# The first load of a streaming cosine-similarity kernel, split into four strided transfers

## Chip, core, metric

One core of one Trainium2 chip. The metric is the device time of one launch in microseconds; the median over runs is given.

## What is computed

For 8192 rows of 8192 float32 values in x and y, the cosine of each pair of rows:

```python
x_norm = np.linalg.norm(x, axis=1, keepdims=True)
y_norm = np.linalg.norm(y, axis=1, keepdims=True)
return np.sum(x * y, axis=1) / (x_norm.squeeze() * y_norm.squeeze() + 1e-8)
```

Each element is used once or twice and never again: 537 MB have to be read, and nothing can be reused.

## The kernel before

The core streams x and y through three buffers of 128 partitions x 64 KB ("slots"). A group is 256 rows, 2 rows per partition, so that each partition receives one unbroken run of 65,536 bytes. ScalarE squares and sums, VectorE multiplies and sums x*y, TensorE only relays semaphores in the loop. The first load is moved by a hook into the program's opening block, ahead of the opening barrier, so that the stream begins as early as it can. The parts that matter (cuts marked):

```python
def first_load_and_last_wait(nc):
    ...
    load = next(i for i in body.instructions if i.opcode == "DMACopy")
    assert not load.sync_info.on_wait
    ...
    body.instructions = [i for i in body.instructions if i.name != load.name]
    opening.instructions = head[:at] + [load] + head[at:]
...
def load(src, m):
    return nc.sync.dma_start(out=slots[m % SLOTS], in_=src).then_inc(landed[m % SLOTS], 16)
...
load(xg[0, 0], 0)          # 128 partitions x 64 KB: moved ahead of the opening barrier
load(yg[0, 0], 1)
load(xg[0, 1], 2)
...
with nc.tensor.Fori(0, R):
    for m in range(2 * SLOTS):
        take(nc.tensor, landed[m % SLOTS], 16)
        nc.tensor.sem_inc(for_act, 1)
        nc.tensor.sem_inc(for_dve, 1)
```

Of the kernel before, what the change touches and what calls it, by code (L numbers as in the profile page):

```python
# [15 lines left out]
def first_load_and_last_wait(nc):  # L16


    blocks = nc.m.functions[0].blocks
    body = next(b for b in blocks if any(i.opcode == "DMACopy" for i in b.instructions))  # L20
    load = next(i for i in body.instructions if i.opcode == "DMACopy")
    assert not load.sync_info.on_wait
    opening = blocks[0]
    head = list(opening.instructions)
    at = 1 + next(n for n, i in enumerate(head)
                  if i.opcode == "ISA" and i.engine == load.engine)
    body.instructions = [i for i in body.instructions if i.name != load.name]
    opening.instructions = head[:at] + [load] + head[at:]



    closing = blocks[-1]
    for b in blocks:
        waits = [i for i in b.instructions
                 if i.sync_info and any(
                     "stored" in (w.ant_name or "") for w in i.sync_info.on_wait)]
        if waits:
            b.instructions = [i for i in b.instructions if i.name not in {w.name for w in waits}]
            closing.instructions = waits + list(closing.instructions)
# [25 lines left out]
def kernel(  # L65
# [5 lines left out]
):  # L71
    nc = tc.nc
    nc.at_finalize(first_load_and_last_wait)
    P = nc.NUM_PARTITIONS
    n_rows, K = x.shape
# [13 lines left out]
    xg = x[0:G * 2 * P, :].rearrange("(r a p j) k -> r a p (j k)", a=SLOTS, p=P, j=2)  # L89
# [17 lines left out]
    slots = [sb.tile([P, 2 * K], FP32, name=f"slot{s}") for s in range(SLOTS)]  # L107
# [18 lines left out]
    def sem(name):  # L126
        return tc.alloc_semaphore(name)

    landed = [sem(f"landed{s}") for s in range(SLOTS)]
    for_act, for_dve = sem("for_act"), sem("for_dve")  # L130
    squared, x_squared, y_squared, partial, used = (
# [6 lines left out]
    def take(engine, s, n=1):  # L138
        engine.wait_ge(s, n).then_inc(s, -n)  # L139
# [9 lines left out]
    def load(src, m):  # L149
        return nc.sync.dma_start(out=slots[m % SLOTS], in_=src).then_inc(landed[m % SLOTS], 16)  # L150
# [16 lines left out]

    with tc.tile_critical():  # L168

        load(xg[0, 0], 0)  # L170
        load(yg[0, 0], 1)
        load(xg[0, 1], 2)

# [8 lines left out]
            load(src[g // SLOTS, g % SLOTS], m)  # L182


        with nc.tensor.Fori(0, R):
            for m in range(2 * SLOTS):
                take(nc.tensor, landed[m % SLOTS], 16)
                nc.tensor.sem_inc(for_act, 1)
                nc.tensor.sem_inc(for_dve, 1)
# [18 lines left out]
        with nc.vector.Fori(0, R) as r:  # L208
# [20 lines left out]
            out=ident, in_=ident, compare_op=ALU.not_equal, fill=1.0, base=0,  # L229
# [42 lines left out]
        def flat(t):  # L272
            return t.rearrange("p q r c -> p q (r c)")
# [10 lines left out]
        for b in range(NB):  # L284
# [8 lines left out]
            for n, p in enumerate(pieces[b]):  # L293
# [4 lines left out]
                else:  # L298
                    dve.wait(*marks)
                    m_base = dve.done(nc.vector.tensor_reduce(  # L300
                        out=base, in_=parts, axis=AX.X, op=ALU.add))
# [24 lines left out]
                if b == last and n == 4:  # L326
# [3 lines left out]
                        out=bnorm[:, :, 0:last], in_=bsum[:, 0:2, 0:last], func=ACTF.Sqrt))  # L330
                    m_den = reciprocal(bnorm[:, :, 0:last], bden[:, 0:last], m_norm, m_sum)
            if b in manys and b != last:
                dve.wait(*marks)
                m_sum = dve.done(nc.vector.tensor_reduce(
                    out=bsum[:, :, b:b + 1], in_=parts, axis=AX.X, op=ALU.add))
            freed[b] = marks
            if b == 0:
# [3 lines left out]
                    out=gnorm, in_=flat(gsum)[:, 0:2], func=ACTF.Sqrt))  # L341
# [3 lines left out]
                    out=gden, in0=flat(gsum)[:, XY], in1=gden))  # L345
                rows = []
                for j in range(2):
# [3 lines left out]
                        out=t, in_=gden[:, j:2 * G:2], identity=ident))  # L351
# [3 lines left out]
            if b == 2:  # L355
                act.wait(*rows)
                nc.scalar.dma_start(
                    out=out[0:G * 2 * P].rearrange("(g q) -> g q", q=2 * P),
                    in_=orow.rearrange("g p j -> g (p j)")).then_inc(stored[0], 16)
# [4 lines left out]
            out=bnorm[:, 0, last:], in_=base[:, XX:XX + 1], func=ACTF.Sqrt))  # L364
        act.wait(m_fin)
        m_yn = act.done(nc.scalar.activation(
            out=bnorm[:, 1, last:], in_=fin, func=ACTF.Sqrt, bias=base[:, YY:YY + 1]))
# [6 lines left out]
            out=bden[:, last:], in0=bnorm[:, 1, last:], scalar1=bnorm[:, 0, last:],  # L374
# [10 lines left out]
            out=out.rearrange("(t p) -> t p", p=P)[nt - NB:, :], in_=orl).then_inc(  # L385
# [33 lines left out]
```

## Time and profile before

| | before |
|---|---|
| time, median of 6 runs | 1249.34 us (1249.20 to 1249.48) |
| span of the profiled run | 1247.6 us |
| share of the span that the load queue keeps 16 DMA engines busy | 99.6% |
| ACT, DVE busy | 73%, 56% |
| one run of 64 KB on one DMA engine (median of 7,680 records) | 2.420 us |

Two things to know for reading what follows. A DMA engine's record is one run of 64 KB (7,680 records of 65,536 bytes; the last blocks are cut smaller, and a semaphore write has a record of its own, 4 bytes and 8 to 14 ns in the kernel before), and in the windows view a record counts, with its whole length and all its bytes, in the window in which it starts. So in a window that contains the starts of just 16 runs, one per engine, the mean length of a run is the DMA share times the width of the window, and the number of runs is GB/s times the width divided by 65.5 KB. And a share above 1.00 in a narrow window is therefore no error. Lengths of single runs, where the text names them, are from the same transfer records of the trace.

### The profile page before, as it was taken

Reading aid. Unit: us, or ns where it says so; the run is one execution under the profiler, and the core shown is the slowest. Engines: PE = TensorE matmul, PEld = TensorE weight load, DVE = VectorE, ACT = ScalarE, POOL = GpSimd, SP = SyncE. Lnnn points to the kernel's source line nnn. Section 1 sums busy time; section 2 is a strip of 40 time slices with the busy share of each in tenths; the row PEclk is TensorE's granted clock in tenths of the full one; section 3 lists DMA queues with packets and bytes.
Section 4 is the critical chain, followed back from the end, with each engine's and each line's share of the span. In section 5 each row is a group of like instructions: output and inputs, shape, how many; then the busy total and the mean of one; then the engine's idle time right before and its main releaser. Section 6 shows DMA issues by size and latency. Waiting matters only on the chain. (4 is left out here: it accounts for less than half of the span.)

```text
span 1247.6 us, 1785 instructions
## 1 busy us (share of the span) xinstructions
PE 1.3 (0%) x4; PEld 0.3 (0%) x4; DVE 698.2 (56%) x252; ACT 916.9 (73%) x285; POOL 0.8 (0%) x8
## 2 busy tenths in 40 slices
PE   0000000000000000000000000000000000000000
PEld 0000000000000000000000000000000000000000
DVE  1654576545765447654467544675446755457566
ACT  3686776867768668677686776867868668677888
POOL 0000000000000000000000000000000000000000
DMA  9999999999999999999999999999999999999998
GB/s 435 431 414 435 437 437 437 437 435 435 433 412 437 437 437 437 437 437 435 435 424 420 437 437 437 437 437 437 433 433 412 437 437 437 437 437 437 418 425 335
DMA packets 11575, 536.93 MB, mean 430 GB/s; under 512 B 1299, under 2 KB 1845, under 8 KB 2613
## 3 DMA queue, kind: packets, MB, share of 16 engines
q1 hardware_dynamic: 11528, 536.88, 99.6%
q10 hardware_dynamic: 45, 0.03, 0.0%
q14 instruction: 2, 0.02, 0.0%
HBM read 536.87 MB, written 0.03 MB: 430 GB/s over the span
## 5 line engine op out<-in xcount | busy, mean ns | idle before, releaser
L142 ACT ACTIVATE junk<-slot 128x8192 uint8<-128x8192 f32 (+4 forms) x138 | 900.8, 6528 | 326.2 <-ACTq L139 320.5
L145 DVE CUSTOM_DVE_ANT_0 slot<-slot,slot 128x4096 f32<-128x4096 f32 (+1 forms) x60 | 391.1, 6556 | 452.4 <-DVEq L139 452.4
L212 DVE COPY side<-slot 128x4096 f32<-128x4096 f32 x30 | 132.8, 4428 | 71.7 <-DVEq L139 71.7
L145 DVE CUSTOM_DVE_ANT_0 side<-side,slot,part 128x4096 f32<-128x4096 f32 x30 | 134.6, 4488 | 0.0
L145 DVE CUSTOM_DVE_ANT_0 slot<-slot 128x8192 f32<-128x8192 f32 (+3 forms) x5 | 29.6, 5944 | 20.4 <-ACT junk L142 12.7
L142 ACT ACTIVATION_READ_ACCUMULATOR junk<-slot (+1 forms) x138 | 25.7, 186 | 0.0
L145 DVE CUSTOM_DVE_ANT_0 vjunk<-slot 128x384 uint8<-128x384 f32 (+4 forms) x8 | 6.8, 886 | 1.0 <-DMA slot<-in_y_dram 1.0
L145 DVE DVE_READ_ACCUMULATOR2_ANT gsum<- x60 | 6.7, 112 | 0.0
L145 DVE DVE_READ_ACCUMULATOR2_ANT part<- 128x1 f32 x30 | 2.5, 83 | 0.0
L192 ACT ACT_TABLE_LOAD x1 | 1.3, 1283 | 1.0 <-SPq L168 1.0
L350 PE MATMUL side<-ident,gden 128*30 128x128 f32 x2 | 0.6, 395 | 1196.9 <-DVE gden L344 1196.9
L194 ACT ACT_TABLE_LOAD x1 | 1.3, 1283 | 0.1
L145 DVE DVE_READ_ACCUMULATOR2_ANT parts<- 128x1 f32 x11 | 0.9, 82 | 0.0
L353 DVE COPY orow<-side 30x128 f32<-30x128 f32 x2 | 0.5, 279 | 0.6 <-PE side L350 0.6
L371 ACT COPY dots<-side 4x128 f32<-4x128 f32 x1 | 0.3, 254 | 0.7 <-PE side L369 0.7
L145 DVE CUSTOM_DVE_ANT_0 vjunk<-slot,base 128x384 uint8<-128x384 f32 x1 | 0.6, 619 | 0.1
L381 DVE TENSOR_TENSOR orl<-side,dots 4x128 f32<-4x128 f32 x1 | 0.3, 279 | 0.5 <-PE side L379 0.5
L270 DVE RECIPROCAL gden<-gden 128x60 f32<-128x60 f32 x1 | 0.5, 529 | 0.0
L350 PEld LDWEIGHTS side<-ident,gden 128*30 128x30 f32 x2 | 0.1, 107 | 1196.8 <-issue 1196.8
L369 PE MATMUL side<-ident,bsum 128*4 128x128 f32 x1 | 0.4, 373 | 46.9 <-DVE bsum L145 46.9
L379 PE MATMUL side<-ident,bden 128*4 128x128 f32 x1 | 0.4, 374 | 0.0
L340 ACT ACTIVATE gnorm<-gsum 128x120 f32<-128x120 f32 x1 | 0.3, 302 | 0.0
(25 smaller groups left out, 4.4 us busy)
## 6 DMA issues: line engine op xcount, KB each, us to landing
slot<-in_x_dram SPq DMA_DIRECT2D x3, 4096.0 KB, 29.9
slot<-in_y_dram SPq DMA_DIRECT2D x2, 4096.0 KB, 32.2
slot<-in_y_dram SPq DMA_DIRECT2D x1, 2368.0 KB, 35.8
slot<-in_x_dram SPq DMA_DIRECT2D x1, 1984.0 KB, 32.3
slot<-in_y_dram SPq DMA_DIRECT2D x1, 1728.0 KB, 39.4
slot<-in_y_dram SPq DMA_DIRECT2D x1, 1600.0 KB, 35.7
slot<-in_x_dram SPq DMA_DIRECT2D x1, 1088.0 KB, 37.9
slot<-in_y_dram SPq DMA_DIRECT2D x1, 640.0 KB, 40.2
```

Of the source, the lines that this page charges most:

```text
L142: return nc.scalar.activation(out=into, in_=src, func=ACTF.Square, accum_out=acc)
L145: return nc.vector.tensor_tensor_reduce(out=into, in0=a, in1=b, scale=1.0, scalar=init, op0=ALU.mult, op1=ALU.add, accum_out=acc)
L192: nc.scalar.memzero(dummy).then_inc(squared, 1)
L194: nc.scalar.sqrt(out=dummy, in_=dummy).then_inc(squared, 1)
L212: nc.vector.tensor_copy(out=side, in_=xt[:, CUT:])
L270: return dve.done(nc.vector.reciprocal(out=den, in_=den))
L340: m_norm = act.done(nc.scalar.activation(out=gnorm, in_=flat(gsum)[:, 0:2], func=ACTF.Sqrt))
L350: mk = pe.done(nc.tensor.transpose(out=t, in_=gden[:, j:2 * G:2], identity=ident))
L353: rows.append(dve.done(nc.vector.tensor_copy(out=orow[:, :, j], in_=t)))
L369: m_xy = pe.done(nc.tensor.transpose(out=psl[0], in_=bsum[:, XY, :], identity=ident))
L371: m_dots = act.done(nc.scalar.copy(out=dots, in_=psl[0]))
L379: mk = pe.done(nc.tensor.transpose(out=psl[1], in_=bden, identity=ident))
```

## The change

A load of 128 partitions is 128 runs, 8 for each of the 16 DMA engines: the 16 semaphore writes of the first load come at 20.97 to 21.57 us, at the end of the eighth generation of 16 runs, and ACT's first square follows at 22.36. The change wants the engines to start sooner by giving each only one run in the first transfer, then one, two and four more. The transfers are strided; each engine is meant to stay within a set of 8 partitions of its own by that. They are partitions 0, 8, .. 120; then 4, 12, .. 124; then 2, 6, .. 126; then 1, 3, .. 127. Three of them count on a semaphore of their own, for which TensorE waits once.

```diff
-    load = next(i for i in body.instructions if i.opcode == "DMACopy")
+    loads = [i for i in body.instructions if i.opcode == "DMACopy"][:4]
...
-    opening.instructions = head[:at] + [load] + head[at:]
+    opening.instructions = head[:at] + loads + head[at:]
...
+    first = sem("first")
...
-        load(xg[0, 0], 0)
+        for start, step in ((0, 8), (4, 8), (2, 4), (1, 2)):
+            nc.sync.dma_start(
+                out=slots[0][start::step], in_=xg[0, 0, start::step]).then_inc(
+                    landed[0] if step == 2 else first, 16)
...
+        nc.tensor.wait_ge(first, 48)
         with nc.tensor.Fori(0, R):
```

More of the change, by code (lines that the diff above doesn't have):

```diff
@@ L20, in first_load_and_last_wait @@
     body = next(b for b in blocks if any(i.opcode == "DMACopy" for i in b.instructions))
-    load = next(i for i in body.instructions if i.opcode == "DMACopy")
-    assert not load.sync_info.on_wait
+    loads = [i for i in body.instructions if i.opcode == "DMACopy"][:4]
+    assert not any(i.sync_info.on_wait for i in loads)
     opening = blocks[0]
@@ L25, in first_load_and_last_wait @@
     at = 1 + next(n for n, i in enumerate(head)
-                  if i.opcode == "ISA" and i.engine == load.engine)
-    body.instructions = [i for i in body.instructions if i.name != load.name]
-    opening.instructions = head[:at] + [load] + head[at:]
+                  if i.opcode == "ISA" and i.engine == loads[0].engine)
+    body.instructions = [i for i in body.instructions if i.name not in {k.name for k in loads}]
+    opening.instructions = head[:at] + loads + head[at:]
     closing = blocks[-1]
```

## The prediction

Passages that no trace or run of this case bears out are cut from the text, and the cuts are marked. Two of its numbers stand as estimates alone: that a first transfer with an eighth of the runs would win half of the measured loss of 0.87 us and a little more, 0.5 us; and that the runs of rival 2, the "conflict" of its last paragraphs, would take twice the measured 2.42 us, 4.84 us. That a faster stream isn't to be had was not shown either; the prediction counts on none.

> **What bounds the kernel now.** I read the page first. Every one of the 40 slices of the span has the DMA engines at 90% or more except the last, while DVE is busy 56% and ACT 73%; the queue of the loads holds 99.6% of the time of 16 engines:
>
> ```profile
> span 1247.6 us, 1785 instructions
> DMA  9999999999999999999999999999999999999998
> q1 hardware_dynamic: 11528, 536.88, 99.6%
> HBM read 536.87 MB, written 0.03 MB: 430 GB/s over the span
> ```
>
> Next, the table of windows over the loop (columns that matter here: the stretch in us, and at the end of the line the DMA share and GB/s; a transfer record counts in the window in which it starts). Share 1.00 in all: no engine waits for a free buffer anywhere in the loop. So time can be won only before the stream of loads runs, by a faster stream, or after it.
>
> ```profile
> 25.00:325.00 300.00, 0.00 (x0) 0.00 (x0) 167.17 (x53) 222.84 (x63) 0.00 (x0) 1.00 1.00 433
> 325.00:625.00 300.00, 0.00 (x0) 0.00 (x0) 165.87 (x55) 218.48 (x63) 0.00 (x0) 1.00 1.00 433
> ```
>
> The DMA records of the trace give the unit: a run of one partition (2 rows of x, 65,536 bytes) is one record, 7,680 of them, median 2.420 us, which is 27.1 GB/s for one of 16 engines. All of x and y is 536.87 MB / 65,536 / 16 = 512 such runs per engine, 512 x 2.420 = 1239.0 us. Of the span of 1247.6 us only about 8.6 us is anything else.
>
> The change touches the head. The timeline and the fine windows of it:
>
> ```profile
> 0.00 0.41 SPq L150 DMA_DIRECT2D slot<-in_x_dram  x1
> 1.07 0.33 SPq L150 DMA_DIRECT2D slot<-in_y_dram  x1
> 22.36 7.03 ACT L142 ACTIVATE junk<-slot 128x8192 uint8<-128x8192 f32 x1 [18.25 <-ACTq L139]
> ```
>
> ```profile
> 1.00:1.25 0.25, 0.00 (x0) 0.00 (x0) 0.00 (x0) 0.23 (x1) 0.20 (x1) 1.00 8.78 2884
> 1.25:1.50 0.25, 0.00 (x0) 0.00 (x0) 0.00 (x0) 0.25 (x1) 0.02 (x2) 1.00 3.04 1049
> 1.75:2.00 0.25, 0.00 (x0) 0.00 (x0) 0.00 (x0) 0.25 (x1) 0.13 (x3) 1.00 0.62 262
> 4.00:4.50 0.50, 0.00 (x0) 0.00 (x0) 0.00 (x0) 0.11 (x1) 0.00 (x0) 1.00 4.54 1966
> 4.50:5.00 0.50, 0.00 (x0) 0.00 (x0) 0.00 (x0) 0.00 (x0) 0.00 (x0) 1.00 0.30 131
> ```
>
> Read the first line so: 2884 GB/s x 0.25 us = 0.72 MB = 11 runs begin there; their time is 8.78 x 0.25 x 16 = 35.1 us, 3.19 us each. Four more begin by 1.50 (3.04 us each), and the sixteenth engine begins only at 1.98 and needs 2.48. From the second run on (15 begin before 4.50: 4.54 x 0.5 x 16 / 15 = 2.42 us) everything runs at 2.42. So the first runs take up to 1.0 us more than any later ones. By the records the engines begin their second runs between 4.06 and 4.66 us, mean 4.33. Had all begun at 1.04 and taken 2.42, it would be 3.46: the head loses **0.87 us in the mean and 1.20 on the last engine**, and the last one matters, since a load has landed only when all 16 have.
>
> Last, the end, where the chain of waits and the timeline of ACT show that a shift of the stream is a shift of the end: the last blocks wait for DMA, and then compute runs on without a gap.
>
> ```profile
> 1222.16 19.49 DMA slot<-in_y_dram
> 1241.65 0.02 issue
> 1241.67 0.54 DVE vjunk L145
> ```
> ```profile
> 1237.89 1.27 ACT L142 ACTIVATE junk<-slot 128x1280 uint8<-128x1280 f32 x1 [0.26 <-DMA slot<-in_y_dram]
> ```
>
> [...] The trace of before has no addresses. What it does show is that engines phase-locked within 0.6 us all run at 27.1 GB/s[...].
>
> **The change part by part.**
> - Three more issues at the start. An issue of 128 runs took 0.33 to 0.52 us of SP; four take about 1.5 us instead of 0.41, so the opening barrier falls some 1.1 us later, and so do the ACT table loads (from 1.02) and the issues of y and the second x (from 1.07). Needed: y's descriptors at about 21 us, ACT at 22.36. Slack 19 us: **0**. A queued run lasts 2.42 us, far longer than the 0.4 us to the next issue, so no engine runs dry between the four: **0**.
> - Semaphore writes: one per engine and transfer, records of 9 ns. Three more: **+0.03 us**.
> - TensorE waits once for 48 before its loop. The fourth transfer is queued last on every engine and so ends last; the wait is long over or ends with it: under 0.1 us, and that on a consumer, not on the stream: **0**.
> - The gain. Fifteen engines start at 1.04 to 1.44 and yet end their first run 0.5 to 1.0 us late, the sixteenth starts 0.9 us late and is not slowed. [...] Possible is at most the 0.87 mean, 1.20 last. [...] I take half of the mean and a little more for the last engine: **-0.5 us**.
> Sum: 1249.4 - 0.5 + 0.03 = **1248.9 us**.
>
> **The rivals.**
> 1. *The slowness of the first runs is a cold start[...].* Against it: the engine that started last took 2.48. For it: that one started when the others were already warm. Then the gain is 0 to 0.2: 1249.2 to 1249.4.
> 2. [...] the first two transfers, and in step the third and fourth too, run [...] 4.84 instead of 2.42 us a run. All 8 runs: +19.4 us, **1268**; only the first two: +4.8 us, **1254**. Nothing later can win this back, since the stream has no slack. [...] Against it: the change is made so that each engine keeps its 8 partitions, which somebody seems to have had reason for[...]. I give this 4 in 10.
> 3. *The load is hidden anyway*, as ACT waits for it only at 22.36: rejected, because it's the stream, not that wait, that sets the end.
>
> **Range and chances.** Without a conflict 1248.2 (all of 1.2 us) to 1249.5; with one 1254 to 1269. The point is where the more likely branch lies, 1248.9; a range for 8 in 10 has to hold the other branch as well, 1248.2 to 1268.5. 2% faster would be 1224.4, under the 1239.0 of the runs alone: 0.01. 2% slower is 1274.4, beyond even the full conflict: 0.03. Within 2%: 0.96.
>
> **What would show it.** Right: in the fine windows all first runs begin by about 1.5 us and last nearer 2.4 than 3.2; the second runs begin at 3.6 to 4.2; ACT's first square begins at about 21.8 instead of 22.36; the final DVE pieces are 0.5 us earlier. Cold start: first runs still about 3.1 us. Conflict: runs of about 4.8 us and half of 437 GB/s up to 10 us or to 40 us, ACT's first square near 27 to 41, and the whole timeline late by the same. What would make the prediction wrong otherwise: issues of strided transfers that cost much more than 0.5 us on SP, so that engines run dry between them, or runs cut into smaller pieces by the stride.

## The result, and the profile after

| | before | after |
|---|---|---|
| time, median of 6 runs each | 1249.34 us | 1254.67 us (1254.42 to 1254.92) |
| span of the profiled run | 1247.6 us | 1252.5 us |
| load queue, share of 16 engines | 99.6% | 99.6% |

The ratio is 1.0043, 95% interval 1.0030 to 1.0056. It is the mean time of one kernel's runs over that of the other's of the same rounds, so not quite the ratio of the medians. The change costs 5.3 us: within 2%, outside the noise, and in the direction that was not the point of the prediction.

The page's busy row does not show where. The DMA engines are "90% or more" in 39 of 40 slices in both kernels. The row below it does. This is its GB/s row for the kernel before (its DMA row is in the prediction), then both rows for the kernel after (slices of about 31 us):

```profile
GB/s 435 431 414 435 437 437 437 437 435 435 433 412 437 437 437 437 437 437 435 435 424 420 437 437 437 437 437 437 433 433 412 437 437 437 437 437 437 418 425 335
```
```profile
DMA  9999999999999999999999999999999999999998
GB/s 362 427 429 427 433 433 435 435 435 435 435 435 435 435 435 435 433 433 435 425 429 427 435 431 435 435 435 435 435 435 435 435 435 435 435 433 433 413 429 335
```

The first slice moved 362 GB/s instead of 435, by engines that the page has at 90% or more all the time: (435 - 362) x 31.3 us = 2.3 MB less, and 2.3 MB at 435 GB/s is 5.3 us. The fine windows of the kernel after, one for each generation of 16 runs:

```profile
1.40:1.90 0.50, 0.00 (x0) 0.00 (x0) 0.00 (x0) 0.00 (x0) 0.00 (x0) 1.00 9.61 2097
5.60:6.90 1.30, 0.00 (x0) 0.00 (x0) 0.00 (x0) 0.85 (x2) 0.00 (x0) 1.00 3.79 807
10.50:11.80 1.30, 0.00 (x0) 0.00 (x0) 0.00 (x0) 0.00 (x0) 0.00 (x0) 1.00 2.29 807
13.80:14.70 0.90, 0.00 (x0) 0.00 (x0) 0.00 (x0) 0.00 (x0) 0.00 (x0) 1.00 2.69 1165
```

Each line has 16 runs (2097 x 0.50 / 65.5 = 16, and so on). The runs of the first transfer take 9.61 x 0.50 = 4.80 us, those of the second 4.91 (the window gives 3.79 x 1.30 = 4.93 and includes the short semaphore writes), the first ones of the third transfer 2.96 (2.98 by the window, again with semaphore writes), and from then on 2.42 as before (2.69 x 0.90 = 2.42). So two transfers, the two of 16 partitions, ran at half rate (4.80 and 4.91 us a run beside 2.42). By the records the account is complete: mean start of the first runs 1.54 us instead of 1.23 (+0.31), first run 4.80 instead of 3.11 (+1.69), second 4.91 instead of 2.42 (+2.49), third 2.96 instead of 2.42 (+0.54), sum 5.03 us. The rest of the kernel is the old one, later. Here are the issues and ACT's first square, and the end of the chain, of the kernel after:

```profile
0.00 2.53 SPq L173 DMA_DIRECT2D slot<-in_x_dram  x4
3.42 0.39 SPq L151 DMA_DIRECT2D slot<-in_y_dram  x1
27.61 7.03 ACT L143 ACTIVATE junk<-slot 128x8192 uint8<-128x8192 f32 x1 [21.14 <-ACTq L140]
```
```profile
1225.38 21.24 DMA slot<-in_y_dram
1246.62 0.02 issue
1246.64 0.54 DVE vjunk L146
```

ACT starts 27.61 - 22.36 = 5.25 us later, the final DVE pieces 1246.64 - 1241.67 = 4.97 us later. Of the profiled pair's difference in time (1254.58 - 1249.41 = 5.17 us) and of the medians' 5.33, the 4.97 us leave some 0.2 to 0.4 us that are not placed by the trace.

### The profile page after: what moved, and what is told of

Its sections match the earlier page's. It is cut to its first block, busy times and chain, and to the rows that moved or that the text cites. A ratio compares the mean times of both kernels' runs of the same rounds, so it can differ in the third digit from the quotient of the medians.

```text
span 1252.5 us, 1788 instructions
## 1 busy us (share of the span) xinstructions
PE 1.3 (0%) x4; PEld 0.3 (0%) x4; DVE 698.2 (56%) x252; ACT 916.9 (73%) x285; POOL 0.8 (0%) x8
## 3 DMA queue, kind: packets, MB, share of 16 engines
q1 hardware_dynamic: 11576, 536.88, 99.6%
```

## The experiments

Theory: how long a run takes depends on which partitions the transfer writes, and two sets of 16 partitions 8 apart (0, 8, .. 120 and 4, 12, .. 124) are slow ones. Rivals: small transfers are slow as such; rows that are read 512 KB apart are slow to read.

The expectations named theories of why a set of partitions is slow, and from them said which runs would be slow. No trace of this case shows the mechanisms, so they are cut, with the cuts marked. What is left of an expectation are the lengths and times that it said, estimates in multiples of the measured 2.42 us; where two or three alternatives follow each other, each belonged to a theory of its own.

### Three transfers, of 32, 32 and 64 partitions

```diff
-        for start, step in ((0, 8), (4, 8), (2, 4), (1, 2)):
+        for start, step in ((0, 4), (2, 4), (1, 2)):      # and 3 hoisted loads, wait for 32
```

> First load in three strided transfers, partitions 0,4,..,124 then 2,6,..,126 then 1,3,..,127 (32, 32, 64)[...]. [...] no run of about 4.9 us is left, the first runs take about 3 us and all later ones 2.42; time 1248.8 to 1250, that is 4.7 to 5.9 us under the changed kernel. Rival, small transfers as such are slow (their set-up or their completion): the two first transfers still cost about 2 us per run, some 1252 to 1255. Rival, rows read from DRAM at a pitch of 512 KB collide: the pitch is now 256 KB, which that theory leaves open; no clear expectation.

Measured: 1250.11 us (5 runs, 1249.78 to 1250.26) beside 1249.32 for the kernel before, ratio 1.0006 with an interval of 0.9992 to 1.0019. Correct. The windows of its first two generations:

```profile
1.30:2.30 1.00, 0.00 (x0) 0.00 (x0) 0.00 (x0) 0.00 (x0) 0.00 (x0) 1.00 3.09 1049
4.40:5.00 0.60, 0.00 (x0) 0.00 (x0) 0.00 (x0) 0.60 (x1) 0.00 (x0) 1.00 4.05 1748
```

First runs 3.09 us, second 2.43: the half-rate runs are gone with the transfers of 16 partitions 8 apart, and about 4.6 us with them. Of the 0.8 us that are left over the kernel before, the trace places 0.34: the mean start of the second runs is 4.67 us instead of 4.33, and as the first runs are no longer than before, it is the stream that starts later. This already says that the gain hoped for does not exist either: with 2 runs per engine in the first transfer instead of 8, the first run takes as long as ever (3.09, before 3.11).

### The same sizes, adjacent partitions

```diff
-        for start, step in ((0, 8), (4, 8), (2, 4), (1, 2)):
-            ... out=slots[0][start::step], in_=xg[0, 0, start::step] ...
+        for lo, hi in ((0, 16), (16, 32), (32, 64), (64, 128)):
+            ... out=slots[0][lo:hi], in_=xg[0, 0, lo:hi] ...
```

> First load in the same four sizes (16, 16, 32, 64) but of adjacent partitions: 0 to 15, 16 to 31, 32 to 63, 64 to 127. [...] a run takes about 4 x 2.42 = 9.7 us in the first two transfers; the third and fourth [...] 4.84 us a run. Sum 9.7 + 9.7 + 9.7 + 19.4 = 48.5 us instead of 19.4 for the load: about 1278, at least 1265[...]. Rival, small transfers as such are slow: the same as the changed kernel, 1254 to 1255, runs of 4.9 us. Rival, DRAM pitch of 512 KB: rows now lie 64 KB apart, so 1249 to 1250.

Measured: 1278.99 us (4 runs), ratio 1.0238, interval 1.0222 to 1.0254. The windows, one for each of the first four generations:

```profile
1.00:1.80 0.80, 0.00 (x0) 0.00 (x0) 0.00 (x0) 0.00 (x0) 0.00 (x0) 1.00 10.57 1311
8.60:10.30 1.70, 0.00 (x0) 0.00 (x0) 0.00 (x0) 0.00 (x0) 0.00 (x0) 1.00 5.48 617
17.90:19.60 1.70, 0.00 (x0) 0.00 (x0) 0.00 (x0) 0.00 (x0) 0.00 (x0) 1.00 3.34 617
24.00:25.00 1.00, 0.00 (x0) 0.00 (x0) 0.00 (x0) 0.00 (x0) 0.00 (x0) 1.00 5.12 1049
```

10.57 x 0.80 = 8.46 us for the first run, 9.29 by the records for the second, 5.6 and 5.1 after that, in the transfer of 32 adjacent partitions. Expected were 9.7, 9.7, then 4.84. A run of 16 adjacent partitions takes 3.8 times 2.42 us in the second transfer, one of 32 adjacent partitions 2.1 to 2.3 times. The whole is 29.7 us slower; the expectation had said about 29. Sizes and count of the transfers are those of the changed kernel. But two things differ from it, the partitions and the rows of DRAM that are read; the next run has the rows of this one with the partitions of the changed kernel, and the comparison of the two is the strongest single result.

### The same partitions, adjacent rows of DRAM

```diff
+        for start, step, lo, hi in ((0, 8, 0, 16), (4, 8, 16, 32), (2, 4, 32, 64), (1, 2, 64, 128)):
+            ... out=slots[0][start::step], in_=xg[0, 0, lo:hi] ...
```

> The changed kernel's partitions of SBUF (0,8,.. then 4,12,.. then 2,6,.. then 1,3,..), but each transfer reads adjacent rows of DRAM[...]. The rows of the first group are then wrong on purpose (256 of 8192 results). [...] nothing changes, runs of 4.9 us in the first two transfers, time 1254 to 1255.5. Rival, DRAM pitch: runs of 2.4 to 3.1 us, time 1249 to 1250.[...]

Measured: 1254.57 us (4 runs), the same as the changed kernel. Its output is wrong, which doesn't matter for the time. The windows of its first two generations:

```profile
1.40:2.20 0.80, 0.00 (x0) 0.00 (x0) 0.00 (x0) 0.00 (x0) 0.00 (x0) 1.00 5.91 1311
5.70:6.70 1.00, 0.00 (x0) 0.00 (x0) 0.00 (x0) 0.77 (x2) 0.00 (x0) 1.00 5.01 1049
```

First runs 5.91 x 0.80 = 4.73 us, second 4.99 by the records. Where the rows are read from makes no difference to the time (1254.57 and 1254.67 us): the DRAM rival is out. The rival of small transfers as such allows this time, but for the run of adjacent partitions, of the same sizes, it had said 1254 to 1255 us. And beside the run of adjacent partitions, which reads the same rows with transfers of the same sizes, only the partitions written differ: 1278.99 us there, 1254.57 here. What it is about the partitions that costs the time, these runs don't show.

### Probes

The other nine runs are the kernel before with one extra transfer into the third buffer, whose own load then waits for it. For example:

```diff
         load(xg[0, 0], 0)
+        nc.sync.dma_start(out=slots[2][0:106:7], in_=xg[0, 1, 0:106:7]).then_inc(probed, 16)
         load(yg[0, 0], 1)
+        nc.sync.wait_ge(probed, 16)
         load(xg[0, 1], 2)
```

The extra runs stand in the records right behind the first load, at 21 us, when all engines run in step at 2.42 us. All probes give right results. Their times, 1252 to 1258 us, include the extra bytes and the wait and say little; one look each, so their state is unknown, but the verdict is in lengths of single runs, which are steady at 2.42 us elsewhere in the same trace.

**16 partitions 7 apart from 0**:

> The kernel before, with one extra transfer of 16 partitions 7 apart (0, 7, .., 105) into the third buffer right behind the first load, when the engines already run in step; the third buffer's own load waits for it. [...] of the 16 extra runs exactly 4 take clearly more than 2.42 us (up to 4.9), 12 take 2.42. Rival, small transfers as such: all 16 equally slow. Rival, DRAM pitch (448 KB here): none slow, or all. The time itself says little: the extra 1 MB and the wait cost at least 2.4 us.

A miss:

```profile
20.80:21.60 0.80, 0.00 (x0) 0.00 (x0) 0.00 (x0) 0.00 (x0) 0.00 (x0) 1.00 5.30 1311
```

All 16 runs took 3.8 to 4.6 us, mean 4.23 by the records, where 4 slow and 12 fast ones had been expected. I formed two other theories, and the next probes were to tell them apart; their mechanisms stayed without evidence.

**8 partitions, 4 apart from 0**, the control:

> The probe of 16 partitions 7 apart slowed all 16 runs (3.8 to 4.6 us)[...]. This probe is the control: an extra transfer of 8 partitions 4 apart (0, 4, .., 28)[...]. [...] the 8 extra runs take 2.42 us and nothing is slow. If they are slow all the same, then a transfer of few partitions is slow as such.

All 8 extra runs, and the other engines' runs beside them, took 2.42 us:

```profile
21.00:21.70 0.70, 0.00 (x0) 0.00 (x0) 0.00 (x0) 0.00 (x0) 0.00 (x0) 1.00 3.47 1498
```

3.47 x 0.70 = 2.43 us with the semaphore writes. Few partitions alone do no harm.

**8 partitions, 4 apart from 4**:

> As the control, with partitions 4, 8, .., 32[...]. [...] the 8 extra runs take clearly more than 2.42 us, 3.5 to 4.9. [...] 2.42 us, apart from up to 0.7 us at the start[...].

The runs at that moment took 2.44 to 2.57 us, the next 2.57 to 2.77. Nothing near 3.5: of the 1.1 us and more that the first alternative added to 2.42, some 0.2 are to be seen (0.35 in the slowest run).

**8 partitions, 5 apart from 0**:

> As the control, with partitions 0, 5, .., 35[...]. [...] all 8 extra runs take 3.8 to 4.9 us, and perhaps the other 8 engines' first runs of y too. [...] 4 runs of 2.42 us and 4 slow ones. [...] 2 slow runs, 6 of 2.42.

Exactly two runs were slow, 4.14 and 4.22 us; six took 2.42, and so did the other eight engines. The windows show it by the starts of the next runs:

```profile
21.00:21.50 0.50, 0.00 (x0) 0.00 (x0) 0.00 (x0) 0.00 (x0) 0.00 (x0) 1.00 5.29 2097
23.50:23.90 0.40, 0.00 (x0) 0.00 (x0) 0.40 (x1) 0.40 (x1) 0.00 (x0) 1.00 5.33 2294
25.20:25.50 0.30, 0.00 (x0) 0.00 (x0) 0.30 (x1) 0.30 (x1) 0.00 (x0) 1.00 1.22 437
```

Sixteen begin by 21.5; fourteen (2294 x 0.40 / 65.5) go on before 23.9 and two (437 x 0.30 / 65.5) after 25.2. That is the third alternative, which neither of my two new theories had expected.

**16 partitions, 3 apart from 0**:

> 16 partitions 3 apart (0, 3, .., 45)[...]. [...] all 16 runs take [...] about 6.5 to 7.3 us. [...] as in the probe 7 apart, so about 4.2 us as there. [...] 3 runs near 2.4, 4 near 4.8, 9 near 7.3.

All 16 were slow:

```profile
21.00:21.50 0.50, 0.00 (x0) 0.00 (x0) 0.00 (x0) 0.00 (x0) 0.00 (x0) 1.00 14.50 2097
```

They took 6.7 to 7.8 us, mean 14.50 x 0.50 = 7.25, three times 2.42 (7.26). Here the first alternative was right, all of them slow, though it was not with 8 partitions.

**16 partitions, 4 apart from 28**:

> The extra transfer behind the first load again, 16 partitions 28, 32, .., 88[...]. [...] all 16 runs take 3.8 to 4.9 us[...]. [...] as with 8 partitions: 2 slow runs, 14 of 2.4 to 2.7.

Two slow runs, 5.0 and 5.5 us, and fourteen of 2.7 to 2.9. That is nearest to the second alternative, but the rest lost too, and more in their next runs: 13 of the 14 that followed took 3.1 to 3.3 us and one 5.08.

**16 partitions, 7 apart from 11** (spacing of the first probe):

> As before, 16 partitions 7 apart from 11 on (11, 18, .., 116): the same spacing as the probe in which all runs were slow[...]. [...] 2.4 to 2.7 us, no run over 3. [...] all about 4.2 us, as in the probe 7 apart from 0.

No slow run at all:

```profile
21.00:21.60 0.60, 0.00 (x0) 0.00 (x0) 0.00 (x0) 0.00 (x0) 0.00 (x0) 1.00 4.05 1748
```

4.05 x 0.60 = 2.43 us in the mean, with the spacing and the number of partitions of the probe that took 4.23. The second alternative is refuted, and so is "16 partitions are slow as such". What separates the two probes is the start, and with it the partitions that are written (the rows that are read made no difference above), and nothing else that I varied.

**16 partitions, 4 apart from 24**:

> Open since the other probes: [...] slows two runs of 16, [...] (7 apart from 0) and [...] (3 apart) slowed all 16. [...] with the spacing of the one that behaved: 24, 28, .., 84[...]. [...] 4 slow runs of 4 to 5.5 us, 12 of 2.4 to 2.8. [...] all 16 take 3.8 to 5 us. Which it is, no theory of mine says beforehand.

All 16 slow, 4.1 to 4.8 us:

```profile
20.90:21.50 0.60, 0.00 (x0) 0.00 (x0) 0.00 (x0) 0.00 (x0) 0.00 (x0) 1.00 7.51 1748
```

7.51 x 0.60 = 4.51 us. Beside the probe from 28 only one partition of the sixteen is another, 24 for 88 (the others have moved up a place in the transfer), and there two runs were clearly slow and here all sixteen. Each was seen in one transfer only. Why, I can't say; no run here tells it, and it stays open. The changed kernel doesn't depend on it: its own two sets were measured, 4.80 and 4.91 us.

**16 partitions, 4 apart from 32, ahead of everything**: 32, 36, .. 92, issued before the first load.

> What the change meant to do[...]: an extra transfer of 16 partitions, 32, 36, .., 92[...], into the third buffer, ahead of everything. Theory COLD START: the first run on every engine is slow[...] however little is queued behind it; the 16 runs take 2.9 to 3.4 us (2.4 for an engine that begins late), as the first runs of the kernel before. Theory of the prediction[...]: they take about 2.4 us[...]. Both: none takes 4.2 to 5.4 us as the first runs of the changed kernel did, though this too is a transfer of 16 partitions.

```profile
1.40:2.20 0.80, 0.00 (x0) 0.00 (x0) 0.00 (x0) 0.74 (x1) 0.47 (x3) 1.00 3.73 1311
```

3.73 x 0.80 = 2.98 us in the mean, with most of the early starters between 2.9 and 3.4. COLD START had the lengths right: one run per engine does not start up quicker than eight (2.98 and 3.11 us). The prediction's estimate, that with fewer runs in the first transfer the first one gets shorter, had not. The run is what the change wanted to do, done without runs of 4.2 us and more (all next runs begin by 5.1 us), and it wins nothing; it also begins at 1.41 us instead of 1.04.

One rival is not met by this run alone. The hook moves only the extra transfer, so the full loads are issued right behind it (SP is busy with them from 1.51 to 2.37 us), and it could be that work that slows the first runs. The records speak against it: the four engines that began at 1.98 us or later, beside the second of these issues, took 2.49 to 2.76 us, and in the kernel before, where full loads are issued at 55.31 and 59.99 us into the running stream, the runs of that moment take 2.42 to 2.43. What it is that is cold in the first microseconds, no run tells.

No version came out that beats the kernel before. The best split, 32, 32 and 64, is 0.8 us behind in the medians; by the interval that is within noise, though all five of its runs lie above all nine of the kernel before. A split needs a gain from the first run, and there is none.

## Why the prediction was right or wrong

The measured 1254.67 us lies in the range; the point, 1248.9, is 5.8 us off, on the wrong side of the kernel before. By its own steps:

- **The bound**: right. The loop of the kernel after has a share of 1.00 and 433 GB/s as before, and what the head lost, nothing won back. (The full slices of the page before run from 412 to 437 GB/s; the 300 us windows, 433, are the better figure.)
- **Three more issues, cost 0**: half right. They cost more than the 1.5 us estimated, 2.53 us on SP for the four (0.57 to 0.64 each by the records, before 0.41), and the ACT table loads moved from 1.02 to 3.37 us. That was hidden, as said. What was not hidden is that the first data came later, mean start 1.54 us instead of 1.23: +0.31 us, a term missing from the sum. It goes with the length of the first issue: 0.64 us here and the first data at 1.42; 0.42 us and 1.03 with adjacent partitions.
- **Semaphore writes, TensorE's wait**: right, nothing to see (records of 8 to 20 ns). The semaphore writes of the four transfers come at 5.65 to 6.86, 10.56 to 11.78, 16.27 to 17.04 and 25.94 to 26.71 us: the fourth does end last, and what TensorE waits for is there 9.7 us before the load's end.
- **The gain of 0.5 us**: this step failed. It was the estimate that fewer runs in the first transfer would make the first run shorter: the first run takes 2.98 us with one run per engine queued, 3.09 with two, 3.11 with eight. The number queued at the start does not matter, and the 0.5 us do not exist. Rival 1 had the lengths right; what is cold stays open. The engine that started last and took 2.48 was the evidence I weighed most, and it fits a cold start just as well, as the text itself noted.
- **Rival 2, the conflict**: given 4 in 10, and it is what happened. Its small form, "only the first two: +4.8 us, 1254", was right in which transfers run at half rate (4.80 and 4.91 us) and in its sum: the run lengths added 1.69 + 2.49 + 0.54 = 4.72 us. That the sum fits so well is in part luck, for the prediction had 2.42 more on each of two runs, and nothing on a third. The sign that it named came true too: ACT's first square at 27.61 us, where 27 to 41 was said. That the range holds 1254.67 at all is owed to this branch; the point's own steps could not have given it. Its large form, the third and fourth in step too, was wrong: from the second runs of the third transfer on the changed kernel is back at 2.42 us, and a first transfer of 32 partitions 4 apart runs at 2.43 us (second runs; the first ones 3.09). Which engine writes which partition, the records don't show.

The choice between the branches rested on "somebody seems to have had reason for" the set of 8 partitions. What stood against it had no trace behind it either. What was missing was a measurement of the sets of partitions themselves, and the runs then gave it: in the second generation a run takes 9.29 us with 16 adjacent partitions, 4.91 with 16 partitions 8 apart, 2.43 with 32 partitions 4 apart. The intention in someone's diff is not evidence about the chip. One probe of 16 partitions 8 apart before the prediction would have been.

## What to carry to other kernels

When a kernel is bound by a saturated stream of DMA, look at GB/s and at the length of one run, not at the busy share: a run of 4.91 us is recorded as busy throughout, just as one of 2.42 is (the load queue's share is 99.6% in both kernels). When a load is cut by partitions, measure the length of one run for the very set of partitions of each piece; here runs of 16 partitions 8 apart and of 16 adjacent ones took about 2 and 3.8 times as long as those of the full load (4.91 and 9.29 us beside 2.42), and the full stream behind did not win the loss back. And before optimizing a slow start, measure whether it depends on the thing that you mean to make smaller.

## What the runs measured

- The length of a 64 KB run (2.42 us in the full load) by the partitions that a transfer writes. At rate: 16 partitions 7 apart from 11 (2.43 us), 8 partitions 4 apart from 0 (2.42) and from 4 (2.44 to 2.57), 32 partitions 4 apart (2.43) and 64 partitions 2 apart (2.42). Slow: 16 partitions 7 apart from 0 (mean 4.23), 4 apart from 24 (4.51), 8 apart (4.91), 3 apart from 0 (7.25), 16 adjacent ones (9.29). Two runs slow: 8 partitions 5 apart from 0 (4.14 and 4.22, the others 2.42), 16 partitions 4 apart from 28 (5.0 and 5.5, the others 2.7 to 2.9).
- The first 64 KB run on each engine after the start takes 2.98 to 3.11 us in the mean instead of 2.42 where the set of partitions isn't a slow one, whether 1, 2 or 8 runs per engine are in the first transfer; engines that began at 1.98 us or later took 2.48 to 2.76.
- In the first microseconds an issue of a strided transfer of 16, 32 or 64 partitions occupies SP for 0.57 to 0.64 us in the changed kernel, one of a full load 0.33 to 0.52 in the kernel before. Three strided ones (32, 32, 64) took 1.85 us together, four of adjacent partitions (16, 16, 32, 64) 1.98, the four strided ones of the changed kernel 2.53.
- The profile's busy share includes all of the time that a slow run takes: at half rate all 16 engines are still shown as busy throughout.
